# Modulation rows in a pool of their own, their sums queued behind evictions, and weights traced ahead of the forms

## The chip, the cores and the metric

The kernel runs on one core of a Trainium2 chip. The metric is the device time of one execution in microseconds (us). A core has five engines that run side by side, each working through its own instruction list in order: TensorE (PE, matrix products; PEld is its loading of stationary weights), VectorE (DVE, elementwise work), ScalarE (ACT, functions and copies), GpSimd (POOL) and SyncE (SP, which here issues nearly all DMA transfers). Products are accumulated in PSUM and brought back to SBUF by DVE or ACT; that step is called an eviction.

## The reference

A trunk of two layers works on one sequence of 512 tokens with 1024 channels. Layer 0 mixes tokens with a grouped complex state-space model (S5), layer 1 with forgetting attention (FoX, 16 heads of 64). Each is followed by a gated ConvFFN with 2816 hidden channels. So there are four sub-layers, numbered 0 to 3 in the kernel (S5, FFN0, FoX, FFN1), and each has this frame:

```python
shift, scale, gate = split(silu(c) @ ada_w + ada_b, 3)   # 3072 numbers from the 1024 of c
hn = rmsnorm(h, g) * (1 + scale) + shift
h = h + gate * sublayer(hn)
```

The attention adds to each logit the cumulated `log_sigmoid` of a forget logit. The FFN is `(silu(causal_conv3(a)) * b) @ w_down` with `a, b = split(hn @ w_up)`. All data are float32.

## The kernel before

**Products.** Activations lie with channels on the 128 partitions and tokens along the free dimension. Each float32 operand is split into a rounded part (`hi`, fp32r, made by ACT in line 286) and a remainder (`lo`, made by DVE in line 287; this is `put_parts`), and a product is three matmuls: hi·hi, hi·lo, lo·hi (`mms`, line 303). So each weight tile of 128x1024 costs one ACT copy (`w_hi`) and one DVE subtraction (`w_lo`) before TensorE can finish with it. Five buffers of each hold weights ahead of use (`WB`), three hold the raw loads.

**The FFN.** Its 22 hidden tiles f are handled in four groups of 6, 5, 6 and 5 (`GROUPS`); the down-projection of one group runs beside the up-projection of the next. A hidden tile is either *whole* (two up-products in halves, 96 matmuls with 256 columns) or *quartered* (`quarters`, line 523 on): seven products of a Winograd form, 84 such matmuls (line 558), for which DVE forms sums of weight quarters (line 529). The quartered tiles also need four sums of activations, the *forms* (`forms_x`: line 492 for the plain activations, line 498 for the differences), traced step by step beside the first whole tiles. `WHOLE_TILES` names the whole tiles of FFN0 and FFN1.

**The modulation sums.** For S5's shift and scale, and for FFN0's, TensorE multiplies `ada_w` by c (`ada_pe`). The other 64 rows of 128 values are made by DVE: `ada_units` loads a 128x1024 tile of transposed `ada_w` (`ada_raw`, 512 KB, by SP in line 254) and reduces its product with the row of c (`ada_c`) in line 255. Such a sum is called a sum or a row here. Generators with these sums stand in `self.bg`, and `tick(n)` traces n of them. `ada_pool` (line 242) opens room for the row of c and for 4 (S5), 2 (FFN0) or 3 (FoX) loads in the pool of the stage, and loads the row of c there, three times in all.

**Where the sums are traced.** S5's gate: three behind each of the last three GLU products (`ticks=3`). FFN0's gate, FoX's shift, scale and gate: in FFN0, by `SUMS`, 1 for each of tiles 0 to 3 and then 2. FFN1's shift, scale and gate: four behind each of two FoX value blocks (`self.tick(4)` in `fox_values`) and one behind each of the 16 q and k products.

**The order of work.** The start of S5 is ordered by hand. All else is ordered by a planner at compile time: it takes the program's order as priority, runs it against its own costs, and puts on each engine's list the first instruction that it expects to be ready. An instruction may so be listed far from its place in the program. A `behind(...)` block adds that an instruction must follow a named one on its engine's list.

**The forget logits.** `fox_values` computes the value tiles and, beside the first, the 16 forget logits `ft`. `log_forget` then runs a chain of about 40 small DVE instructions on them (lines 706 to 732, last result `lf_out`); `cumsum` transposes it on TensorE (line 1302), scans it on DVE (line 1306) and sends it through DRAM to the heads. On TensorE's list the transposes stand behind the value products, and the q and k products (line 303 again) behind the transposes.

Of the kernel before, what the change touches and what calls it, by code (L numbers as in the profile page):

```python
# [45 lines left out]
ROWS_FROM = 0  # L46
GROUPS = (6, 5, 6, 5)
TAIL = 4
WHOLE_TILES = (0, 1, 2, 3, 6, 8, 10, 12, 14, 16, 18), (0, 1, 2, 3)
SUMS = (1, 1, 1, 1, 2, 2) + (2,) * 12  # L50
FIRST = (("c", (KT,)), ("s5_prm", (3, G // 2)), ("s5_eye", (64,)))
REST = (
    ("ident", (P,)), ("ada_b", (4, 24)), ("norm_g", (4, KT)), ("final_g", (KT,)), ("cmask", (P,)), ("fox_bf", (NH,)), ("s5_causal", (L,)),
# [10 lines left out]
class Trunk:  # L64
# [6 lines left out]
    def __init__(self, tc, io, ctx):  # L71
        self.tc, self.nc, self.io, self.ctx = tc, tc.nc, io, ctx
        nc = self.nc
        pool = lambda name, bufs, **k: ctx.enter_context(tc.tile_pool(name=name, bufs=bufs, **k))
        self.const = pool("const", 1)
        self.act = pool("act", 1)
        self.wpool = pool("wpool", 3)
        self.tmp = pool("tmp", 2)
        self.small = pool("small", 2)
        self.dram = pool("dram", 1, space=DRAM)  # L80
        self.mm = pool("mm", 4, space=PSUM)
        self.aux = pool("aux", 4, space=PSUM)
        self.bg = []
        self.acc = None
        self.pending = None
        self.rests, self.odd = 0, False

        self.ones = self.const.tile([P, P], F32, name="ones")
        nc.vector.memset(self.ones, 1.0)
        self.sc = self.const.tile([P, KT], F32, name="sc")  # L90
        self.sc32 = self.const.tile([P, KT, 32], F32, name="sc32")

        self.sel = self.const.tile([P, 6], F32, name="sel")
        nc.gpsimd.memset(self.sel, 0.0)
# [144 lines left out]
        nc.scalar.activation(rows, ps, AF.Copy)  # L239
        nc.sync.dma_start(self.cd, rows)  # L240

    def ada_pool(self, pool, bufs):

        self.bgpool, self.ada_bufs = pool, bufs
        self.crow = pool.tile([P, D], F32, name="ada_c")
        self.nc.sync.dma_start(self.crow, self.cd.rearrange("k p -> (k p)")[None].to_broadcast([P, D]))

    def ada_units(self, i, thirds):

        nc = self.nc  # L250
        for t in thirds:
            for m in range(8 * t, 8 * t + 8):
                w = self.bgpool.tile([P, D], F32, name="ada_raw", bufs=self.ada_bufs)
                nc.sync.dma_start(w, self.io["ada_rows"][i - ROWS_FROM, m])
                nc.vector.tensor_tensor_reduce(  # L255
                    w, w, self.crow, 1.0, self.ada_b[:, i, m:m + 1], ALU.mult, ALU.add, self.par[i][:, m:m + 1]
                )
# [26 lines left out]
    def put_parts(self, hi, lo, src):  # L284
        nc = self.nc
        nc.scalar.activation(hi, src, AF.Copy)  # L286
        nc.vector.tensor_tensor(lo, src, hi.bitcast(F32), ALU.subtract)  # L287

    def weights(self, w, nk, *pool):

# [13 lines left out]
                o, wt, xt[:, cols], start=(k == 0 and n == 0), stop=(k == nk - 1 and n == 2),  # L304
            )

    def product(self, w, ms, nk, x, evac, head=0, tail=0, after=None, ticks=0, halves=HALVES, tail_pool=(), first=None, step=None, apart=False, ready=()):


        ms = list(ms)  # L310
        full = slice(0, S)
        if head:
            wk = first or {m: self.weights(w[m], nk) for m in ms[:head]}
            ps = {m: self.mm.tile([P, S], F32, name="mmp") for m in ms[:head]}
            for c in halves:
                for k in range(nk):
                    for m in ms[:head]:
                        self.mms(ps[m][:, c], wk[m], x, k, nk, c)
                    self.finish_norm((k + 1) * head)
                    if step:  # L320
                        step(3)
            for m in ms[:head]:
                evac(m, ps[m], full)
                self.tick(ticks)
        for m in ms[head:len(ms) - tail]:
            wk = ready[m] if m in ready else self.weights(w[m], nk)
            ps = self.aux.tile([P, S], F32, name="aux") if m in ready else self.mm.tile([P, S], F32, name="mmp")
# [39 lines left out]

    def add_residual(self, i, last=True):
        def evac(m, ps, cols):
            self.nc.vector.scalar_tensor_tensor(  # L370
                self.h[:, m, cols], ps, self.par[i][:, 16 + m:17 + m], self.h[:, m, cols],
                op0=ALU.mult, op1=ALU.add,
            )
            if last:
                self.square(m, cols)
# [213 lines left out]
    def ffn(self, i, l, x, nxt, whole, sums=()):  # L589

        nc, tc = self.nc, self.tc
        with tc.tile_pool(name=f"ffn{l}", bufs=1, reuse_waits="tile") as pool:
            if sums:
                self.ada_pool(pool, 2)
            first = [sum(GROUPS[:q]) for q in range(len(GROUPS) + 1)]
            keep, g = {}, {}

# [45 lines left out]
            todo = []  # L643
            for q, n in enumerate(GROUPS):
                for j, f in enumerate(range(first[q], first[q + 1])):
                    if f == 0:
# [1 line left out]
                        todo.append(self.forms_x(pool, x, b))  # L648
                    elif f in whole:
                        if f > 1:  # L650
                            up([f])
                        for _ in range(4):
                            if todo and next(todo[0], True):
                                todo.pop()
                    else:
# [131 lines left out]
class S5(Trunk):  # L787
# [291 lines left out]
    def s5(self, i, nxt):  # L1079
# [5 lines left out]
        with ExitStack() as stack:  # L1085
# [123 lines left out]
            for m in range(KT):  # L1209
# [24 lines left out]
                if m >= KT - 2:  # L1234
                    parts(m - 2)
            outputs(KT - 1)
            for k in range(KT - 1):
                if k == KT - 2:
                    parts(k)
                glu_head(k, 0)  # L1240
            for k in range(KT - 1):
                glu_head(k, 1)
            parts(KT - 1)
            for p in range(2):
                glu_head(KT - 1, p)
# [2 lines left out]
        with tc.tile_pool(name="s5b", bufs=1, reuse_waits="tile") as pool:  # L1248
# [5 lines left out]
            def glu(m, ps, cols):  # L1254
# [4 lines left out]

            self.product(  # L1260
                self.io["s5_w_glu"], range(HEAD, HEAD + 1), KT, (yhi, ylo), lambda m, ps, cols: gps.update({m: ps}),
                ready=ready,
            )
            for m in range(HEAD + 1):
                glu(m, gps[m], slice(0, S))
            self.ada_pool(pool, 4)
            self.bg = [self.ada_units(i, [2])]
            self.product(self.io["s5_w_glu"], range(HEAD + 1, KT), KT, (yhi, ylo), glu, ticks=3)
            self.load_x(resid)
            self.done()  # L1270
            after, y = nxt
            self.product(self.io["s5_w_out"], range(KT), KT, (zhi, zlo), self.add_residual(i), tail=2, after=after)
        return y


class Kernel(S5):
# [32 lines left out]
    def fox_values(self, pool, x):  # L1309
# [44 lines left out]
        values((0, 1), (0, 1), w)  # L1354
        values((0, 1), (2, 3), w, ((0, 2), (0, 3)))
        lf = self.log_forget(ft, pool)
        self.ada_pool(pool, 3)
        for q in range(2, NV):
            values((q,), range(NB), {q: load(q)})
            self.tick(4)  # L1360
        return lf

    def fox(self, i, x, nxt):
# [11 lines left out]
    def fox_heads(self, pool, x):  # L1375
# [14 lines left out]
        def project(m, ps, cols):  # L1390
            hi, lo = (pool.tile([P, S], F32R, name=n, tag="qk", bufs=QK) for n in ("hi", "lo"))
            if m % 2 == 0:
                sc = HD ** -0.5
                nc.scalar.activation(hi, ps, AF.Copy, scale=sc)
                nc.vector.scalar_tensor_tensor(lo, ps, sc, hi.bitcast(F32), op0=ALU.mult, op1=ALU.subtract)
                qp[m // 2] = hi, lo
            else:
                self.put_parts(hi, lo, ps)
# [103 lines left out]
def build(tc, io, out, stop=None):  # L1502
    with ExitStack() as ctx:
# [97 lines left out]
```

## Time and profile before

| | |
|---|---|
| median of 3 runs | 1236.39 us (1236.01 to 1238.03) |
| the profiled execution, its own time | 1235.54 us |
| its span, first to last instruction | 1233.8 us |
| TensorE busy | 1193.6 us (97%) |
| VectorE busy | 987.3 us (80%) |
| ScalarE busy | 597.2 us (48%) |
| modulation sums on VectorE | 64, 81.7 us |
| mean granted TensorE clock | 0.987 |

The profile times each instruction on its engine. A row of a timeline has the start, the duration, the engine, the line, what is written and read, and in brackets the idle time of the engine before it with what ended that. A row of the windows has a stretch of the span, its length, the busy time of PE, PEld, DVE, ACT and POOL with counts, the granted TensorE clock as a share of full speed, the busy share of the DMA engines and GB/s. A row of waits has the total idle time, the number of waits and the longest. In a row of the chain stand start, duration, what.

### The profile page before, as it was taken

How to read it: one execution, taken by the hardware profiler on the slowest of the kernel's cores; microseconds unless marked ns; L12 is line 12 of the kernel's file. 1: busy time of each engine (PE TensorE's matmuls, PEld its weight loads, DVE VectorE, ACT ScalarE, POOL GpSimd, SP SyncE). 2: the span in 40 equal slices, each digit the busy share in tenths (PEclk: the TensorE clock that was granted, in tenths of full speed). 3: DMA queues.
4: the chain of work that ended last, by engine and by line, in shares of the span. 5: the costliest groups of instructions: out<-in, count | busy, mean ns of one | idle time of the engine just before them, and what ended most of it. 6: DMA issues, size and time to landing. Idle time of an engine off the chain costs nothing.

```text
span 1233.8 us, 21319 instructions
## 1 busy us (share of the span) xinstructions
PE 1193.6 (97%) x8311; PEld 1042.2 (84%) x8311; DVE 987.3 (80%) x1824; ACT 597.2 (48%) x1102; POOL 57.0 (5%) x113
## 2 busy tenths in 40 slices
PE   7999998998999999999998899999989999999997
PEld 2566677898999999999898688888989999999987
DVE  7898977669998986667789777765899888888865
ACT  3544444435543444435443356654456555555543
POOL 0000000000000000000000234331000000000000
PEclk9999999999999999999999899999999999999999
DMA  9677559432566743323538734331313333333331
GB/s 360 225 238 226 140 177 331 158 124 84 184 221 221 241 133 108 107 77 103 181 120 312 244 109 133 128 104 39 101 56 108 117 108 92 116 103 108 103 86 69
DMA packets 73524, 184.92 MB, mean 150 GB/s; under 512 B 23135, under 2 KB 25535, under 8 KB 72399
## 3 DMA queue, kind: packets, MB, share of 16 engines
q1 hardware_dynamic: 73135, 183.04, 45.3%
q8 instruction: 65, 1.06, 0.4%
q10 hardware_dynamic: 288, 0.52, 0.1%
q14 instruction: 36, 0.29, 0.1%
HBM read 176.62 MB, written 6.92 MB: 149 GB/s over the span
## 4 chain that ended last, share of the span: by engine, by line
PE 87%; DVE 7%; DMA 3%; ACT 1%; issue 1%; SPq 0%; POOL 0%; DVEq 0%; ACTq 0%; POOLq 0%
PE mmp L303 44%; PE mmp L558 16%; PE aux L558 6%; PE mmp L1171 4%; PE mmp L1342 2%; PE aux L975 2%; PE aux L1488 2%; PE aux L1471 1%; DVE w_lo L287 1%; PE aux L1064 1%; PE aux L1056 1%; PE mmp L219 1%; DMA ada_raw<-in_ada_rows 1%; PE aux L1441 1%; DVE ada_raw L255 1%
## 5 line engine op out<-in xcount | busy, mean ns | idle before, releaser
L286 ACT ACTIVATE w_hi<-raw 128x1024 fp32r<-128x1024 f32 (+4 forms) x197 | 176.1, 902 | 170.3 <-PE mmp L303 87.6
L287 DVE TENSOR_TENSOR w_lo<-raw,w_hi 128x1024 fp32r<-128x1024 f32 (+4 forms) x197 | 203.5, 1037 | 31.5 <-ACT w_hi L286 30.8
L303 PE MATMUL mmp<-a_hi,w_lo 128*128 128x256 f32 (+1 forms) x632 | 195.2, 310 | 11.5 <-DVE w_lo L287 11.4
L303 PE MATMUL mmp<-a_hi,w_hi 128*128 128x256 f32 (+1 forms) x632 | 197.9, 315 | 0.5 <-DVE conv L614 0.5
L303 PE MATMUL mmp<-a_lo,w_hi 128*128 128x256 f32 (+1 forms) x632 | 194.5, 308 | 0.0
L303 PE MATMUL mmp<-ghi,w_hi 128*128 128x512 f32 (+1 forms) x392 | 143.9, 367 | 0.0
L303 PE MATMUL mmp<-glo,w_hi 128*128 128x512 f32 (+1 forms) x392 | 143.9, 367 | 0.0
L303 PE MATMUL mmp<-ghi,w_lo 128*128 128x512 f32 (+1 forms) x392 | 143.6, 366 | 0.0
L303 PEld LDWEIGHTS mmp<-a_hi,w_lo 128*128 128x128 f32 x632 | 121.1, 192 | 19.3 <-DVE w_lo L287 12.7
L303 PEld LDWEIGHTS mmp<-a_hi,w_hi 128*128 128x128 f32 x632 | 121.3, 192 | 8.6 <-issue 2.6
L303 PEld LDWEIGHTS mmp<-a_lo,w_hi 128*128 128x128 f32 x632 | 121.4, 192 | 5.1
L286 ACT ACTIVATE w_hi<-sums 128x1024 fp32r<-128x1024 f32 x66 | 69.6, 1059 | 57.2 <-DVE sums L529 27.8
L558 PE MATMUL mmp<-w_hi 128*128 128x256 f32 x348 | 96.1, 276 | 0.0
L558 PE MATMUL mmp<-w_lo,w_hi 128*128 128x256 f32 x348 | 96.1, 276 | 0.0
L558 PE MATMUL mmp<-w_hi,w_lo 128*128 128x256 f32 x348 | 96.0, 276 | 0.0
L255 DVE CUSTOM_DVE_ANT_0 ada_raw<-ada_raw,ada_c,rest 128x1024 f32<-128x1024 f32 x64 | 81.7, 1283 | 12.6 <-DMA ada_raw<-in_ada_rows 12.4
L287 DVE TENSOR_TENSOR w_lo<-sums,w_hi 128x1024 fp32r<-128x1024 f32 x66 | 80.1, 1220 | 12.1 <-ACT w_hi L286 11.0
L370 DVE SCALAR_TENSOR_TENSOR h<-mmp,par,h 128x512 f32<-128x512 f32 (+1 forms) x92 | 62.1, 677 | 32.1 <-PE mmp L303 32.0
L303 PEld LDWEIGHTS mmp<-ghi,w_lo 128*128 128x128 f32 x392 | 73.6, 188 | 12.3
L303 PEld LDWEIGHTS mmp<-ghi,w_hi 128*128 128x128 f32 x392 | 73.6, 188 | 11.2
L303 PEld LDWEIGHTS mmp<-glo,w_hi 128*128 128x128 f32 x392 | 73.6, 188 | 11.1
L558 PEld LDWEIGHTS mmp<-w_lo,w_hi 128*128 128x128 f32 x348 | 65.3, 188 | 0.0
(312 smaller groups left out, 2829.7 us busy)
## 6 DMA issues: line engine op xcount, KB each, us to landing
raw<-in_w_up SPq DMA_DIRECT2D x88, 512.0 KB, 3.6
ada_raw<-in_ada_rows SPq DMA_DIRECT2D x64, 512.0 KB, 4.7
raw<-in_ada_w SPq DMA_DIRECT2D x32, 512.0 KB, 6.5
raw<-in_w_down SPq DMA_DIRECT2D x32, 384.0 KB, 3.3
raw<-in_w_down SPq DMA_DIRECT2D x32, 320.0 KB, 3.0
nf<-nfd SPq DMA_DIRECT2D x8, 1152.0 KB, 5.7
raw<-in_fox_qk SPq DMA_DIRECT2D x16, 512.0 KB, 4.2
h<-in_x SPq DMA_DIRECT2D x8, 512.0 KB, 5.5
```

The lines of the kernel that those rows point to most:

```text
L219: self.last_mm = nc.tensor.matmul(ps[32 * qq:32 * qq + 32, :], self.sc32[:, k, :], w[:, q * S:(q + 1) * S], start=(step is steps[0]), stop ...
L255: nc.vector.tensor_tensor_reduce(w, w, self.crow, 1.0, self.ada_b[:, i, m:m + 1], ALU.mult, ALU.add, self.par[i][:, m:m + 1])
L286: nc.scalar.activation(hi, src, AF.Copy)
L287: nc.vector.tensor_tensor(lo, src, hi.bitcast(F32), ALU.subtract)
L303: self.last_mm = self.nc.tensor.matmul(o, wt, xt[:, cols], start=(k == 0 and n == 0), stop=(k == nk - 1 and n == 2),)
L370: self.nc.vector.scalar_tensor_tensor(self.h[:, m, cols], ps, self.par[i][:, 16 + m:17 + m], self.h[:, m, cols], op0=ALU.mult, op1=ALU.add,)
L558: self.last_mm = nc.tensor.matmul(o, wt[:, k], xt[:, k], start=(first and k == 0 and n == 0), stop=(k == H - 1 and n == 2), skip_group_che ...
L975: nc.tensor.matmul(ps[g2][:, j, cols], x[rows, a + j, r].rearrange("p c j -> p (c j)"), self.rr[rows, planes, q, :], start=(j == 0 and r = ...
L1056: nc.tensor.matmul(yp[g2][:, k, :], t[:, g].rearrange("p c i -> p (c i)"), u[:, g, :], start=(k == 0), stop=False, skip_group_check=True,)
L1171: nc.tensor.matmul(ps, w[m][:, k, :], x[:, k], start=(k == 0), stop=(k == KT - 1))
L1342: self.last_mm = nc.tensor.matmul(ps[q, b][:, :n], xt[:, k, tb], wt, start=(k == 0 and i == 0), stop=(k == KT - 1 and i == 2),)
L1488: nc.tensor.matmul(pv[:, c * P:], self.v[:, hp, k, r].rearrange("p t d -> p (t d)"), pp[:, r, c + 3 * k:NB + 3 * k, :].rearrange("p b t -> ...
```

## The change

- One pool `ada` lives from the start to the end, with the row of c and two loads of `ada_raw`. The row of c is loaded once, after the S5 outputs (`load_c`); `ada_pool` is gone.
- S5's gate sums are traced earlier: three after the first part of the GLU head, two after its second part, held behind the last step of the S5 scan, and one behind each of the last three GLU products.
- FFN0's gate sums move from FFN0 to S5's output product, two behind each of its tiles (`ticks=2`).
- FFN0 has no sums in tiles 0 to 5 and two in each of tiles 6 to 21; FFN1's gate sums move there from FoX. `fox_values` has none. The q and k products keep one each.
- `self.late` keeps the DVE instruction of the latest eviction (or remainder), and each sum must follow it on DVE's list.
- In both FFNs the weights of the next whole tile are traced ahead of the forms' steps while forms are left, and these get three steps a tile instead of four.
- FFN0 has 10 whole tiles instead of 11, placed otherwise.

```diff
-WHOLE_TILES = (0, 1, 2, 3, 6, 8, 10, 12, 14, 16, 18), (0, 1, 2, 3)
-SUMS = (1, 1, 1, 1, 2, 2) + (2,) * 12
+WHOLE_TILES = (0, 1, 2, 3, 4, 8, 11, 14, 17, 20), (0, 1, 2, 3)
+SUMS = (0,) * 6 + (2,) * 16
...
-        self.bg = []
+        self.bg, self.late = [], ()
...
+        self.ada = pool("ada", 1)
+        self.crow = self.ada.tile([P, D], F32, name="ada_c")
...
-    def ada_pool(self, pool, bufs):
-
-        self.bgpool, self.ada_bufs = pool, bufs
-        self.crow = pool.tile([P, D], F32, name="ada_c")
+    def load_c(self):
+
         self.nc.sync.dma_start(self.crow, self.cd.rearrange("k p -> (k p)")[None].to_broadcast([P, D]))
...
-                w = self.bgpool.tile([P, D], F32, name="ada_raw", bufs=self.ada_bufs)
+                w = self.ada.tile([P, D], F32, name="ada_raw", bufs=2)
                 nc.sync.dma_start(w, self.io["ada_rows"][i - ROWS_FROM, m])
-                nc.vector.tensor_tensor_reduce(
-                    w, w, self.crow, 1.0, self.ada_b[:, i, m:m + 1], ALU.mult, ALU.add, self.par[i][:, m:m + 1]
-                )
+                with self.behind(*self.late):
+                    nc.vector.tensor_tensor_reduce(
+                        w, w, self.crow, 1.0, self.ada_b[:, i, m:m + 1], ALU.mult, ALU.add, self.par[i][:, m:m + 1]
+                    )
...
-        nc.vector.tensor_tensor(lo, src, hi.bitcast(F32), ALU.subtract)
+        self.late = (nc.vector.tensor_tensor(lo, src, hi.bitcast(F32), ALU.subtract).ins,)
...
                     elif f in whole:
                         if f > 1:
-                            up([f])
-                        for _ in range(4):
+                            up([f], ready=ready)
+                            ready = {}
+                        if todo and f + 1 in whole:
+                            self.odd = True
+                            ready = {m: self.weights(self.io["w_up"][l][m], KT) for m in (2 * f + 2, 2 * f + 3)}
+                            self.odd = False
+                        for _ in range(3):
                             if todo and next(todo[0], True):
                                 todo.pop()
...
             outputs(KT - 1)
+            self.load_c()
+            self.bg, self.late = [self.ada_units(i, [2])], (self.scanned,)
             for k in range(KT - 1):
                 if k == KT - 2:
                     parts(k)
                 glu_head(k, 0)
+            self.tick(3)
             for k in range(KT - 1):
                 glu_head(k, 1)
+            self.tick(2)
             parts(KT - 1)
...
-            self.ada_pool(pool, 4)
-            self.bg = [self.ada_units(i, [2])]
-            self.product(self.io["s5_w_glu"], range(HEAD + 1, KT), KT, (yhi, ylo), glu, ticks=3)
+            self.product(self.io["s5_w_glu"], range(HEAD + 1, KT), KT, (yhi, ylo), glu, ticks=1)
             self.load_x(resid)
             self.done()
+            self.bg = [self.ada_units(i + 1, [2])]
             after, y = nxt
-            self.product(self.io["s5_w_out"], range(KT), KT, (zhi, zlo), self.add_residual(i), tail=2, after=after)
+            self.product(self.io["s5_w_out"], range(KT), KT, (zhi, zlo), self.add_residual(i), tail=2, after=after, ticks=2)
...
-        self.ada_pool(pool, 3)
         for q in range(2, NV):
             values((q,), range(NB), {q: load(q)})
-            self.tick(4)
...
-        k.bg = [k.ada_units(1, [2]), k.ada_units(2, [0, 1]), k.ada_units(2, [2])]
+        k.bg = [k.ada_units(2, [0, 1]), k.ada_units(2, [2]), k.ada_units(3, [2])]
         x = k.ffn(1, 0, x, k.norm_mod(2), WHOLE_TILES[0], SUMS)
...
-        k.bg = [k.ada_units(3, [0, 1]), k.ada_units(3, [2])]
+        k.bg = [k.ada_units(3, [0, 1])]
```

The evictions in `add_residual` and of q in the attention's `project` set `self.late` in the same way.

More of the change, by code (lines that the diff above doesn't have):

```diff
@@ L305, in mms, with product @@
             )
-    def product(self, w, ms, nk, x, evac, head=0, tail=0, after=None, ticks=0, halves=HALVES, tail_pool=(), first=None, step=None, apart=False, ready=()):
+    def product(self, w, ms, nk, x, evac, head=0, tail=0, after=None, ticks=0, halves=HALVES, tail_pool=(), first=None, step=None, apart=False, ready=(), spare=False):
         ms = list(ms)
@@ L326, in product @@
             wk = ready[m] if m in ready else self.weights(w[m], nk)
-            ps = self.aux.tile([P, S], F32, name="aux") if m in ready else self.mm.tile([P, S], F32, name="mmp")
+            ps = self.aux.tile([P, S], F32, name="aux") if spare else self.mm.tile([P, S], F32, name="mmp")
             for c in HALVES if apart else (full,):
@@ L369, in evac @@
         def evac(m, ps, cols):
-            self.nc.vector.scalar_tensor_tensor(
-                self.h[:, m, cols], ps, self.par[i][:, 16 + m:17 + m], self.h[:, m, cols],
-                op0=ALU.mult, op1=ALU.add,
+            self.late = (
+                self.nc.vector.scalar_tensor_tensor(
+                    self.h[:, m, cols], ps, self.par[i][:, 16 + m:17 + m], self.h[:, m, cols],
+                    op0=ALU.mult, op1=ALU.add,
+                ).ins,
             )
@@ L592, in ffn @@
         with tc.tile_pool(name=f"ffn{l}", bufs=1, reuse_waits="tile") as pool:
-            if sums:
-                self.ada_pool(pool, 2)
             first = [sum(GROUPS[:q]) for q in range(len(GROUPS) + 1)]
@@ L642, in ffn @@
             )
-            todo = []
+            todo, ready = [], {}
             for q, n in enumerate(GROUPS):
@@ L1261, in s5 @@
                 self.io["s5_w_glu"], range(HEAD, HEAD + 1), KT, (yhi, ylo), lambda m, ps, cols: gps.update({m: ps}),
-                ready=ready,
+                ready=ready, spare=True,
             )
@@ L1394, in project @@
                 nc.scalar.activation(hi, ps, AF.Copy, scale=sc)
-                nc.vector.scalar_tensor_tensor(lo, ps, sc, hi.bitcast(F32), op0=ALU.mult, op1=ALU.subtract)
+                self.late = (
+                    nc.vector.scalar_tensor_tensor(lo, ps, sc, hi.bitcast(F32), op0=ALU.mult, op1=ALU.subtract).ins,
+                )
                 qp[m // 2] = hi, lo
```

## The prediction, made before the change was run

> **What bounds the kernel now.** First the page: its head, the chain that ended last by engine, the sums' group and their loads.
>
> ```profile
> span 1233.8 us, 21319 instructions
> PE 1193.6 (97%) x8311; PEld 1042.2 (84%) x8311; DVE 987.3 (80%) x1824; ACT 597.2 (48%) x1102; POOL 57.0 (5%) x113
> PE 87%; DVE 7%; DMA 3%; ACT 1%; issue 1%; SPq 0%; POOL 0%; DVEq 0%; ACTq 0%; POOLq 0%
> ...
> L255 DVE CUSTOM_DVE_ANT_0 ada_raw<-ada_raw,ada_c,rest 128x1024 f32<-128x1024 f32 x64 | 81.7, 1283 | 12.6 <-DMA ada_raw<-in_ada_rows 12.4
> ...
> ada_raw<-in_ada_rows SPq DMA_DIRECT2D x64, 512.0 KB, 4.7
> ```
>
> TensorE is the bound: 40 us of the span are left that it is not busy. DVE comes next on the chain, and a sum holds DVE for 1.28 us. So I read TensorE's own waits, then its timeline where each long one ends.
>
> ```profile
> PE mmp L303 <- DVE w_lo L287: 11.4, 3, 4.8
> PE mmp L1302 <- DVE lf_out L732: 8.4, 1, 8.4
> ```
>
> ```profile
> 215.27 0.79 PE L303 MATMUL mmp<-a_hi,w_lo 128*128 128x512 f32 x1 [3.48 <-DVE w_lo L287]
> 308.80 0.58 PE L303 MATMUL mmp<-a_hi,w_lo 128*128 128x256 f32 x1 [4.78 <-DVE w_lo L287]
> 681.40 1.01 PE L1302 MATMUL mmp<-rest,lf_out 128*16 128x128 f32 x4 [8.36 <-DVE lf_out L732]
> 917.89 0.41 PE L303 MATMUL mmp<-a_hi,w_lo 128*128 128x256 f32 x1 [3.13 <-DVE w_lo L287]
> ```
>
> Four waits, 19.75 us, all for DVE: A in the last GLU products, B at FFN0's tile 3, C at the forget logits, D at FFN1's tile 3. The windows around them show a second price.
>
> ```profile
> 215.00:222.00 7.00, 6.73 (x23) 5.47 (x24) 5.37 (x8) 1.58 (x2) 0.00 (x0) 0.76 0.50 164
> 222.00:257.00 35.00, 35.00 (x166) 29.39 (x166) 20.77 (x23) 14.95 (x18) 0.00 (x0) 1.00 0.43 148
> 309.00:340.00 31.00, 31.00 (x254) 31.00 (x255) 30.78 (x45) 15.62 (x24) 0.00 (x0) 0.92 0.59 187
> 340.00:600.00 260.00, 260.00 (x1862) 243.09 (x1861) 204.05 (x296) 114.58 (x168) 0.12 (x1) 1.00 0.47 152
> 682.00:700.00 18.00, 18.00 (x87) 14.45 (x86) 12.29 (x18) 4.37 (x5) 2.54 (x2) 0.89 0.86 300
> 700.00:820.00 120.00, 118.86 (x696) 98.62 (x697) 86.72 (x226) 78.62 (x196) 44.62 (x68) 1.00 0.37 124
> 918.00:926.00 8.00, 8.00 (x57) 8.00 (x58) 7.62 (x10) 2.64 (x4) 0.00 (x0) 0.79 0.57 172
> 926.00:960.00 34.00, 34.00 (x294) 33.68 (x293) 33.14 (x49) 22.00 (x36) 0.00 (x0) 1.00 0.32 104
> ```
>
> Behind each wait the granted clock is low. A stretch of busy TensorE at a mean clock c loses length x (1 - c): 7 x 0.24 = 1.7, 31 x 0.08 = 2.5, 18 x 0.11 = 2.0, 8 x 0.21 = 1.7. So A costs 3.5 + 1.7 = 5.2 us, B 4.8 + 2.5 = 7.3, C 8.4 + 2.0 = 10.4, D 3.1 + 1.7 = 4.8; together 27.7.
>
> What DVE did ahead of each release, from its timeline (A, B, D; last column releasers):
>
> ```profile
> 210.34 1.32 DVE L255 CUSTOM_DVE_ANT_0 ada_raw<-ada_raw,ada_c,rest 128x1024 f32<-128x1024 f32 x1
> ...
> 212.75 1.32 DVE L255 CUSTOM_DVE_ANT_0 ada_raw<-ada_raw,ada_c,rest 128x1024 f32<-128x1024 f32 x1
> ...
> 213.95 1.26 DVE L287 TENSOR_TENSOR w_lo<-raw,w_hi 128x1024 fp32r<-128x1024 f32 x1
> ...
> 306.39 1.21 DVE L498 TENSOR_TENSOR sums<-x,x 128x1024 f32<-128x1024 f32 x1
> 307.53 2.35 DVE L287 TENSOR_TENSOR w_lo<-raw,w_hi 128x1024 fp32r<-128x1024 f32 x2
> ...
> 914.88 1.22 DVE L498 TENSOR_TENSOR sums<-x,x 128x1024 f32<-128x1024 f32 x1
> 916.01 0.68 DVE L287 TENSOR_TENSOR glo<-conv,ghi 128x512 fp32r<-128x512 f32 x1
> 916.62 1.22 DVE L287 TENSOR_TENSOR w_lo<-raw,w_hi 128x1024 fp32r<-128x1024 f32 x1
> ```
>
> At A the late weight remainder stands behind sums, at B and D behind the forms. For C, DVE over the whole chain of the forget logits: all of it, then the sums (each counts twice, with its read-out), then remainders and evictions of line 287.
>
> ```profile
> 652.00:681.10 29.10, 27.77 (x75) 0.91 0.87 305
> ...
> 652.00:681.10 29.10, 14.11 (x22) 0.91 0.87 305
> ...
> 652.00:681.10 29.10, 10.57 (x15) 0.91 0.87 305
> ```
>
> Eleven sums took 14.1 of these 29.1 us; what else there is takes 13.7.
>
> **The change, part by part.** *Sums out of the value blocks (C).* Without them DVE's 13.7 us of other work end near 652 + 13.7 = 666. TensorE asked at 681.40 - 8.36 = 673.0, so 7 us of cover remain and the wait goes: -10.4. Late next would be the first scores, which need the scan and two transfers behind the transposes; that is a rival below.
>
> *Sums out of the GLU (A) and FFN0's start (B).* The windows of line 255 alone:
>
> ```profile
> 195.00:214.00 19.00, 7.86 (x12) 1.00 0.86 310
> ...
> 265.00:290.00 25.00, 3.84 (x6) 1.00 0.52 171
> ```
>
> At A the weights would have to be ready 3.5 us sooner. Six sums stood ahead of them; five of S5's eight move forward and at most one or two stay ahead, so at least four, 5.1 us, go: -5.2. At B three sums go, 3.8 us, two tiles' weights come ahead of the forms, and tile 4, now whole, asks DVE for two remainders instead of a quartered tile's sums; 4.8 us are needed: -7.3. Tiles 5, 6 and 7 are now quartered in a row. From 309 to 340 two such tiles in a row kept DVE full (30.78 of 31) and TensorE never idle; a third with sums I price at 0 to 2.6 (its two sums), and take 0.5.
>
> *Where these five go.* Behind the last scan step DVE makes the remainders of the GLU head.
>
> ```profile
> 177.85 4.62 DVE L1198 TENSOR_TENSOR w_lo<-raw,w_hi 128x1024 fp32r<-128x1024 f32 x4
> ```
>
> ```profile
> 185.32 6.51 PE L1201 MATMUL mmp<-a_hi,w_lo 128*128 128x512 f32 x28
> ```
>
> They are ready at 182.5 and read from 185.3 on: 2.9 us of cover. Two or three sums in front take 2.6 to 3.8, so 0 to 1.0 us appear, and more if SP stands before a row whose buffer isn't free with the reads of y queued behind it, at most one landing, 4.7. The room issues nothing itself, and two of three loads of the row of c fall away. I take 0.5, near the case without a blocked queue, since the first two rows find their buffers free.
>
> *FFN0's gate sums in the output product.* Eight, 10.2 us, beside 222 to 257, where DVE has 14.2 us idle and TensorE none: 0.
>
> *One whole tile fewer.* 96 - 84 = 12 matmuls, which this row of the chain has as
>
> ```profile
> 431.84 1.36 PE aux L558 x12
> ```
>
> so -1.4. *Sums in tiles 6 to 21*: 32 in place of 24, spread over the rest of FFN0; 340 to 600 has 56 us of idle DVE and TensorE never idle: 0.
>
> *Attention.* 16 sums behind the evictions of q and k; the trace had one of them after 700. They put DVE at 86.7 + 19.2 = 106 of 120 us. Bounds: -1.1 (the idle time there goes) to +19.2 (all on the path); I take +0.5, nearest to FFN0's row, as DVE keeps 14 us.
>
> *FFN1's start (D).* Weights come ahead of the forms, but DVE's work is the same, and it is full to 960. So the question is what is late next: the first quartered tile's sums.
>
> ```profile
> 924.29 1.23 DVE L287 TENSOR_TENSOR w_lo<-sums,w_hi 128x1024 fp32r<-128x1024 f32 x1
> ```
>
> ```profile
> 930.23 2.49 PE mmp L558 x22
> ```
>
> Ready at 925.5, read by that tile's second product at 930.2 + 1.4 = 931.6: 6.1 us of cover. TensorE would come 4.8 earlier, which leaves 1.3; but tile 3's evictions, four steps of about 0.7 (as the 0.68 at 916.01), also come earlier and stand in front, 2.8. So 0 to 1.5 us come back, or all 4.8 if order wasn't it. I take 1.3: -3.5.
>
> Sum: -5.2 - 7.3 - 10.4 - 3.5 - 1.4 + 0.5 + 0.5 + 0.5 = -26.3. The profiled execution took 1235.5 by its own time and the median is 1236.4; so 1209.2 against the first, 1210 against the second.
>
> [...]
>
> **The rivals.** *FFN1's wait only moves* (for: DVE at 33.14 of 34 behind it; against: 6.1 us of cover): -26.3 + 3.5, 1214.
>
> *The first scores wait.* TensorE's first scores, and what DVE did with them:
>
> ```profile
> 697.69 0.38 PE L1441 MATMUL aux<-hi 64*128 64x256 f32 x2
> ```
>
> ```profile
> 699.96 1.28 DVE L255 CUSTOM_DVE_ANT_0 ada_raw<-ada_raw,ada_c,rest 128x1024 f32<-128x1024 f32 x1 [2.18 <-DMA ada_raw<-in_ada_rows]
> ...
> 701.17 0.28 DVE L1453 CUSTOM_DVE_ANT_0 s<-aux,nf 128x128 f32<-128x128 f32 x1
> ```
>
> For: from the transposes at 681.4 DVE's first score took 19.8 us; transposes at 673 give 693, while TensorE, without the 2.0 of half clock, offers scores 14.3 us behind them, at 687. Against: a sum that waited 2.2 us for its row stood before that score. Price up to 6 us: 1216.
>
> *It doesn't do what it says*: the planner still lists weights late, since a sum is tied to one instruction only. Then the tile alone remains: 1235.
>
> *Rows late at the head of DVE's list* (slower). Eleven of 64 sums waited for their load, 12.4 us, 1.1 each, at up to four buffers; now there are two everywhere, and remainders and evictions queue behind a waiting sum. If all 32 pairs wait 1.1 us and TensorE feels it, +35.2: 1236.4 - 26.3 + 35.2 = 1245. It decides above 26.3 / 32 = 0.8 us a pair. Against: with two buffers FFN0 ran 24 sums, and TensorE had no idle time from 340 to 600.
>
> **How the numbers follow.** Forecast 0.55; FFN1 moves 0.17; first scores 0.13; nothing 0.07; slower 0.08. The likeliest is 1210. Low: all gains without costs, -29.1, give 1207, and 3 us beneath for other short waits: 1204. High: both middle rivals together and the 3 us that a late y or a third sum may add: 1222. Outside lie about 0.17: nothing, slower, and a little of the rest. A measurement of this kernel can tell 0.2%, 2.5 us: faster 0.85 (the first three), same 0.07 (1235 is 1.4 from the median), slower 0.08.
>
> **What would show it.** Right: no wait of TensorE on w_lo or lf_out over 1 us, granted clock 1.00 in the stretches above, value blocks without line 255, 84 x 12 = 1008 quarter matmuls in FFN0, and line 255 spread to FFN0's end. Wrong: waits of line 1201 on w_lo, of line 1441 or 1471 on DVE or POOL, DVE idle for ada_raw well over 12.4 us, or a wait at FFN1's first quartered tile.

## The result, and the profile after

The changed kernel takes 1207.41 us (1205.89 to 1209.27, 4 runs) where the kernel before takes 1236.89 (1236.01 to 1238.03, 4 runs): a ratio of 0.9762, with a 95% interval of 0.9744 to 0.978. The forecast was 1210, in a range of 1204 to 1222. The profiled execution took 1206.57 us by its own time, 29.0 less than the one before.

The page of the changed kernel: its head, the chain that ended last by engine, and the group of the sums, which are now on line 256 (lines of the prediction have moved by one to ten).

```profile
span 1204.6 us, 21290 instructions
...
PE 1184.1 (98%) x8299; PEld 1034.5 (86%) x8299; DVE 994.2 (83%) x1834; ACT 600.7 (50%) x1108; POOL 60.7 (5%) x113
...
PE 83%; DVE 8%; DMA 4%; ACT 2%; issue 2%; POOL 0%; SPq 0%; DVEq 0%; ACTq 0%; POOLq 0%
...
L256 DVE CUSTOM_DVE_ANT_0 ada_raw<-ada_raw,ada_c,rest 128x1024 f32<-128x1024 f32 x64 | 83.6, 1326 | 2.5 <-DMA ada_raw<-in_ada_rows 2.4
```

TensorE is idle for 20.5 us where it was 40.2, has 12 matmuls fewer, and DVE stands idle for rows 2.4 us in place of 12.4. What TensorE still waits for, longest first:

```profile
PE mmp L1116 <- ACT nm_t L1115: 5.8, 1, 5.8
PE mmp L1146 <- DVE a_x L1132: 1.7, 1, 1.7
PE aux L390 <- DVE ssq L365: 1.1, 1, 1.1
```

The first two lie in the first 28 us, and the kernel before had both (6.3 and 1.1). The waits on w_lo and on lf_out, 19.75 us together, are gone. The stages in which A, B, C and D lay, by windows (columns: PE, PEld, DVE, ACT, POOL, then granted clock, DMA share, GB/s); the last but one is the attention, of which more below:

```profile
195.00:222.00 27.00, 27.00 (x121) 22.36 (x120) 25.27 (x29) 15.58 (x23) 0.00 (x0) 1.00 0.80 280
...
260.00:320.00 60.00, 60.00 (x527) 59.75 (x526) 57.07 (x95) 33.08 (x48) 0.00 (x0) 1.00 0.24 78
...
652.00:700.00 48.00, 47.44 (x280) 39.49 (x279) 30.76 (x73) 24.76 (x58) 15.75 (x19) 1.00 0.50 167
674.50:794.50 120.00, 119.44 (x702) 98.86 (x699) 100.34 (x250) 78.52 (x196) 47.85 (x69) 1.00 0.55 181
870.00:960.00 90.00, 89.56 (x732) 87.11 (x732) 87.50 (x120) 53.47 (x79) 0.00 (x0) 1.00 0.30 97
```

The clock is 1.00 in each. The span is 29.2 us shorter, and of that TensorE's idle time makes 19.7, as much as the four waits (19.75), and its busy time 9.5. Of the 9.5, 1.36 are the 12 matmuls of the whole tile, by the price of the prediction (no run took this part alone); 8.1 are left for the half clock behind the four waits, which the prediction had summed to 7.9.

### The profile page after: what moved, and what is told of

It is laid out like the page before. It is cut to its first block, busy times and chain, and to the rows that moved or that the text cites. A ratio compares the mean times of both kernels' runs of the same rounds, so it can differ in the third digit from the quotient of the medians.

```text
span 1204.6 us, 21290 instructions
## 1 busy us (share of the span) xinstructions
PE 1184.1 (98%) x8299; PEld 1034.5 (86%) x8299; DVE 994.2 (83%) x1834; ACT 600.7 (50%) x1108; POOL 60.7 (5%) x113
## 3 DMA queue, kind: packets, MB, share of 16 engines
q8 instruction: 65, 1.06, 0.4%
## 4 chain that ended last, share of the span: by engine, by line
PE 83%; DVE 8%; DMA 4%; ACT 2%; issue 2%; POOL 0%; SPq 0%; DVEq 0%; ACTq 0%; POOLq 0%
PE mmp L304 41%; PE mmp L561 14%; PE aux L561 5%; PE mmp L1351 3%; PE mmp L1177 3%; DVE w_lo L288 2%; PE mmp L1207 2%; PE aux L981 2%; PE aux L1497 2%; PE aux L1480 1%; PE aux L1062 1%; PE aux L1070 1%; DMA raw<-in_w_up 1%; PE mmp L221 1%; DVE sums L532 1%
## 5 line engine op out<-in xcount | busy, mean ns | idle before, releaser
L304 PE MATMUL mmp<-a_hi,w_hi 128*128 128x256 f32 (+1 forms) x600 | 185.9, 311 | 0.0
L304 PE MATMUL mmp<-a_hi,w_lo 128*128 128x256 f32 (+1 forms) x600 | 182.8, 306 | 0.0
L304 PE MATMUL mmp<-a_lo,w_hi 128*128 128x256 f32 (+1 forms) x600 | 182.6, 305 | 0.0
L304 PEld LDWEIGHTS mmp<-a_hi,w_hi 128*128 128x128 f32 x600 | 112.4, 188 | 7.6 <-issue 2.5
L304 PEld LDWEIGHTS mmp<-a_hi,w_lo 128*128 128x128 f32 x600 | 112.5, 188 | 6.4
L304 PEld LDWEIGHTS mmp<-a_lo,w_hi 128*128 128x128 f32 x600 | 112.6, 188 | 4.8
L561 PE MATMUL mmp<-w_hi 128*128 128x256 f32 x360 | 99.6, 277 | 0.2 <-ACT nm_h L568 0.2
L561 PE MATMUL mmp<-w_hi,w_lo 128*128 128x256 f32 x360 | 99.5, 276 | 0.0
L561 PE MATMUL mmp<-w_lo,w_hi 128*128 128x256 f32 x360 | 99.4, 276 | 0.0
L561 PEld LDWEIGHTS mmp<-w_hi 128*128 128x128 f32 x360 | 67.6, 188 | 0.5 <-ACT nm_h L568 0.4
```

Of the source, the lines that this page charges most:

```text
L304: self.last_mm = self.nc.tensor.matmul(o, wt, xt[:, cols], start=(k == 0 and n == 0), stop=(k == nk - 1 and n == 2),)
L561: self.last_mm = nc.tensor.matmul(o, wt[:, k], xt[:, k], start=(first and k == 0 and n == 0), stop=(k == H - 1 and n == 2), skip_group_che ...
```

## The experiments

Twelve kernels were run, each against the kernel before on the same chip. Beside these kernels the median of the kernel before lies at 1234.7 to 1236.9, so they are compared by their ratios: a difference of 0.001 is 1.24 us, and the difference of two ratios is uncertain by about 0.002 to 0.003.

| kernel | what differs | median us | ratio | 95% interval |
|---|---|---|---|---|
| changed kernel | all of the change | 1207.41 | 0.9762 | 0.9744 to 0.978 |
| e1_values | FFN1's gate sums written in the value blocks, not held | 1206.32 | 0.9758 | 0.9743 to 0.9772 |
| e2_nohold | no sum held | 1227.32 | 0.993 | 0.9906 to 0.9954 |
| e3_notahead | no weights ahead of the forms | 1209.62 | 0.9784 | 0.9769 to 0.9799 |
| e4_glu | S5's gate sums back in the last GLU products | 1213.00 | 0.9812 | 0.979 to 0.9835 |
| e1c_forget | 16 sums ahead of the forget logits' chain | 1222.03 | 0.989 | 0.9874 to 0.9906 |
| e6_first | sums back in FFN0's first tiles | 1211.07 | 0.9811 | 0.9793 to 0.9829 |
| e9_four | no weights ahead, four steps of the forms | 1217.26 | 0.9855 | 0.984 to 0.987 |
| e10_holdonly | the kernel before, with the hold alone | 1227.81 | 0.9941 | 0.9926 to 0.9956 |
| e11_fourahead | weights ahead, four steps | 1207.82 | 0.9779 | 0.9766 to 0.9793 |
| i1_seven | seven whole tiles in FFN0 | 1205.55 | 0.9759 | 0.974 to 0.9777 |
| e7_nosums | no sums at all | 1204.41 | 0.976 | 0.9737 to 0.9783 |
| i3_five | five whole tiles in FFN0 | 1217.35 | 0.9852 | 0.9836 to 0.9868 |

**Places without the hold, and the hold without the places.** The first kernel is the changed one with

```
-                with self.behind(*self.late):
+                with self.behind():
```

> The changed kernel with all its places for the sums, but no sum is held behind an eviction or the scan. Theory, the places did it: the planner takes a few sums earlier, no long wait of TensorE comes back, 1207 to 1210. Rival, the hold did it: sums slip in front of the weights wherever a row has landed, in FFN0's first tiles above all, and one or two of the waits of 5 to 10 us come back, 1212 to 1222.

It took 1227.32 (its profiled execution 1230.90): without the hold, 0.017 or some 21 us of the gain are lost. The group of the sums (duration in ns, then first and last start) tells why; first of this kernel, then of the kernel before, then of the changed one.

```profile
L256 DVE CUSTOM_DVE_ANT_0 ada_raw<-ada_raw,ada_c,rest x64: 1271/1281/1337, 141.8 to 497.1; 128x1024 f32<-128x1024 f32 x64
```

```profile
L255 DVE CUSTOM_DVE_ANT_0 ada_raw<-ada_raw,ada_c,rest x64: 1248/1278/1349, 195.6 to 700.0; 128x1024 f32<-128x1024 f32 x64
```

```profile
L256 DVE CUSTOM_DVE_ANT_0 ada_raw<-ada_raw,ada_c,rest x64: 1267/1279/1711, 176.5 to 799.3; 128x1024 f32<-128x1024 f32 x64
```

With a room that is open throughout and no hold, all 64 sums are done by 498 us, those written into the attention too: the planner lists them as early as it can. Eight of them now stand between 254 and 279 us, in the normalization ahead of FFN0, in front of the sum of squares and of the root that TensorE waits for. The longest waits behind the start (first fence) and the two stretches of lowest clock (second, columns as above):

```profile
PE mmp L561 <- ACT nm_h L568: 4.4, 5, 3.0
PE aux L420 <- DVE rs_y L411: 3.9, 2, 3.7
PE aux L390 <- DVE ssq L365: 3.6, 1, 3.6
```

```profile
167.00:179.00 12.00, 11.70 (x61) 10.18 (x62) 12.00 (x20) 4.91 (x10) 0.33 (x4) 0.57 0.31 88
262.00:285.00 23.00, 16.02 (x90) 15.59 (x91) 17.02 (x52) 6.48 (x12) 0.00 (x0) 0.70 0.59 198
```

In the first stretch, the last scan steps of S5, two sums run, at 174.0 and 176.5, and the wait is 1.7 us for ACT and ends at 167.3, so they are not its cause; what is, isn't shown. The 3.0 us on nm_h end at 465.1 in FFN0, 10 us behind a sum that itself stood 2.8 us for its row at the head of DVE's list; over the 64 sums such waits are 13.2 us here and 2.4 in the changed kernel, both with two loads.

The other kernel is the one before, with its places, rooms, tiles and forms, and only the hold added:

```
-                nc.vector.tensor_tensor_reduce(...)
+                with self.behind(*self.late):
+                    nc.vector.tensor_tensor_reduce(...)
...
-        nc.vector.tensor_tensor(lo, src, hi.bitcast(F32), ALU.subtract)
+        self.late = (nc.vector.tensor_tensor(lo, src, hi.bitcast(F32), ALU.subtract).ins,)
```

(and the same in the evictions of the residual and of q).

> The kernel before, with one thing of the change alone: each sum held behind the eviction that was traced last. Its places, its rooms, its tiles and its forms stay. Theory (the hold is most of the change, since unheld sums run as early as their room is open, wherever they are written): A and C shrink or go, D (4.8 us) stays and B in part, two sums still stand ahead of the forms: 1217 to 1224. Rival (places are most of it): lf_out and w_lo are waited for as before, 1230 to 1236.

It took 1227.81, 7.3 us less than before by its ratio and a little above the range expected. Its long waits:

```profile
224.69 0.49 PE L304 MATMUL mmp<-zhi,w_hi 128*128 128x512 f32 x1 [1.99 <-ACT zhi L287]
...
309.11 0.58 PE L304 MATMUL mmp<-a_hi,w_lo 128*128 128x256 f32 x1 [5.50 <-DVE w_lo L288]
...
696.88 1.49 PE L1472 MATMUL aux<-rest,s 128*128 128x128 f32 x4 [3.31 <-POOL s L1463]
...
911.56 0.39 PE L304 MATMUL mmp<-a_hi,w_lo 128*128 128x256 f32 x1 [3.09 <-DVE w_lo L288]
```

C is gone by the hold alone: no wait on lf_out is left. Three sums stand right in front of lf_out, where eleven stood in the 29 us of its chain before, and it is ready at 667.4, 6.1 us ahead of the transposes. But three more stand in front of the scan behind them (674.5 to 678.1), and 3.3 us come back at the first scores, 23 us behind the transposes (673.6), as the second rival of the prediction had it. A has moved to the output product's first operand (zhi), D is as long as it was, and B rather longer. So the hold alone is worth 0.6%, the rest of the change without the hold 0.7%, and both together 2.4%: each needs the other.

**C, the forget logits.** A first attempt put the eight sums back into the value blocks, not held there, and took them out of FFN0 (the edit in part):

```
...
         for q in range(2, NV):
             values((q,), range(NB), {q: load(q)})
+            self.hold = False
+            self.tick(4)
+            self.hold = True
...
```

> The changed kernel, but FFN1's gate sums stand again in the two value blocks of the attention, four behind each and not held, and FFN0 has them no longer. Theory: the sums stand between the steps of the forget logits on VectorE's list, so TensorE's wait at the transposes comes back with its half clock: a wait of 7 to 9 us there and 1207 + 10.4 = 1217 to 1219. Rival, the wait came from other things that changed too (the loads, the order of the weights): under 1 us of wait and 1207 to 1209.

It took 1206.32, against the theory. The windows of line 256 in it say why it is no test of C:

```profile
500.00:560.00 60.00, 15.22 (x24) 1.00 0.60 203
560.00:600.00 40.00, 0.00 (x0) 1.00 0.50 151
600.00:652.00 52.00, 0.00 (x0) 1.00 0.21 72
652.00:681.00 29.00, 3.01 (x4) 1.00 0.49 164
```

(Each sum counts twice, with its read-out.) From 560 on only 16 sums are left, as many as the q and k products have; so the eight written into the value blocks ran before 560, beside FFN0, for the same reason as all sums of the run without the hold. A second attempt holds 16 sums at the logits, and lists them ahead of their chain:

```
+                    self.late = (nc.vector.tensor_tensor(ft[:, b, :], ps[q, b][:, W:W + NH], bf, ALU.add).ins,)
+                    self.asked = self.late
...
+        self.late = self.asked
+        self.tick(16)
         lf = self.log_forget(ft, pool)
```

> The last layer's 16 shift and scale sums move from the attention to the forget logits: held behind the addition that makes the logits, and listed ahead of their chain, so that 11 of them stand in DVE's list between that addition and lf_out (none do in the changed kernel). Theory (C was the sums' place: lf_out was ready 8.4 us before TensorE asked, and 11 sums of 1.25 us take 13.8): TensorE waits about 5 us on lf_out and then has a halved clock for one or two stretches, 2 to 3 us more: 1213 to 1216. Rival (DVE has room there, and TensorE does not feel it once sums are held): no wait, 1206 to 1209.

It took 1222.03, 15.8 us over the changed kernel by ratio: the theory's side, and about twice its size.

```profile
640.00:673.00 33.00, 13.99 (x22) 0.92 0.76 268
...
667.60:678.00 10.40, 4.74 (x14) 0.51 0.67 236
...
673.26 1.01 PE L1311 MATMUL mmp<-rest,lf_out 128*16 128x128 f32 x4 [10.80 <-DVE lf_out L738]
```

The eleven sums take 14.0 us, near the 13.8 expected, but lf_out ends at 673.1, 22.7 us later than in the changed kernel: two sums also waited for their rows (0.69 and 1.78 us), and remainders of weights and of v that stood behind the chain got ahead of it. After the wait of 10.8 the clock stays at half for another 4.5 us, which loses 2.2; a wait of 2.02 us on ssq at 604 (1.05 in the changed kernel) and a stretch of half clock behind it (0.54 from 605.9 to 609.6) lose 2.7 more. Together that is 15.7.

**A, the gate sums of S5.** All eight go back into the last GLU products, held (lines between left out):

```
-            self.bg, self.late = [self.ada_units(i, [2])], (self.scanned,)
...
-            self.tick(3)
...
-            self.tick(2)
...
-            self.product(self.io["s5_w_glu"], range(HEAD + 1, KT), KT, (yhi, ylo), glu, ticks=1)
+            self.bg = [self.ada_units(i, [2])]
+            self.product(self.io["s5_w_glu"], range(HEAD + 1, KT), KT, (yhi, ylo), glu, ticks=3)
```

> The changed kernel, but S5's eight gate sums stand in the last three GLU products again, three behind each, held behind evictions as in the changed kernel. Theory: VectorE makes the weights' remainders there too late again, a wait of 3 to 4 us with half a window of half clock, +5.2: 1212. Rival, being held behind evictions is enough for the remainders to pass: 1207 to 1208.

It took 1213.00, 6.2 us over by ratio, near the theory's price. But the wait is another one:

```profile
223.17 0.50 PE L304 MATMUL mmp<-zhi,w_hi 128*128 128x512 f32 x1 [2.20 <-ACT zhi L287]
224.30 0.50 PE L304 MATMUL mmp<-zlo,w_hi 128*128 128x512 f32 x1 [0.63 <-DVE zlo L288]
...
224.70:228.30 3.60, 3.60 (x11) 0.53 0.87 291
```

Held sums stand behind the remainder that TensorE needs in the GLU, and in front of the elementwise steps that make zhi and zlo, which the output product needs; one of them stood 1.4 us for its row, at 217.1. That is 2.8 us and 1.7 of clock, 4.5 in all.

**B and D, the first tiles of the FFNs.** The change has three parts here: no sums, weights ahead of the forms, and three steps of the forms behind a whole tile in place of four. The prediction read over the third. One kernel leaves out the weights ahead (`if False:` in place of `if todo and f + 1 in whole:`), one takes four steps (`range(4)`), one does both, and one puts the sums back (`SUMS = (1, 1, 1, 1, 2, 2) + (2,) * 12`).

> The changed kernel, but the next whole tile's weights are not traced ahead of the forms; the forms keep three steps a tile. Theory: FFN1's wait at tile 3 comes back in full, 4.8 us, and a part of FFN0's, where no sums stand any more, 0 to 3: 1212 to 1215. Rival, the three steps do it alone: 1206 to 1209 and no wait over 1 us at either place.

It took 1209.62: 2.7 us over the changed kernel by ratio, about what two such ratios can tell apart, and there is no wait on w_lo at any tile 3.

> Four steps of the forms behind each whole tile as before the change, and no weights ahead of them; sums as in the changed kernel. Theory (D was the forms standing ahead of the late weight remainder, and B half so): TensorE waits about 3 us on w_lo at FFN1's tile 3, with 1.7 us of clock behind it, and 1 us or less at FFN0's: 1212 to 1215. Rival (the order of the forms is worth no more than the 2.2 us that the weights alone were): 1208 to 1211.

It took 1217.26, 11.5 us over by ratio, and here both waits are back (timeline, then windows of TensorE alone):

```profile
301.08 0.39 PE L304 MATMUL mmp<-a_hi,w_lo 128*128 128x256 f32 x1 [3.30 <-DVE w_lo L288]
...
607.87 0.61 PE L390 MATMUL aux<-ones,ssq 128*128 128x1 f32 x4 [1.39 <-DVE ssq L365]
...
899.91 0.58 PE L304 MATMUL mmp<-a_hi,w_lo 128*128 128x256 f32 x1 [3.13 <-DVE w_lo L288]
```

```profile
302.50:306.00 3.50, 3.50 (x19) 0.51 0.75 274
609.50:613.50 4.00, 4.00 (x24) 0.57 0.00 2
900.00:903.50 3.50, 3.50 (x17) 0.53 0.53 167
```

D is back to the hundredth (3.13 before, 3.13 here). B is back at 3.30 of its 4.78, though no sum stands there: the theory had given it 1 us or less, and the time lies above its range.

> Four steps of the forms behind each whole tile as before the change, with the weights ahead of them as in the changed kernel: the other half of the run without either, which took 1217.3 with two waits on w_lo of 3.3 and 3.1 us. Theory (three steps in place of four carry B and D, the weights ahead hardly anything): TensorE waits 2 to 3 us on w_lo at tile 3 of each FFN, with a stretch of half clock behind each: 1213 to 1217. Rival (either of the two is enough, each puts tile 3's late remainder ahead of the last forms): no such wait, 1206 to 1210.

The rival is right: 1207.82, 0.0017 over the changed kernel and not told apart from it, with no wait on w_lo. So either of the two is enough, weights ahead or one step less, and the change has both.

> FFN0's sums are spread as before the change (one beside each of tiles 0 to 3, two from tile 4 on), each still held behind an eviction; weights ahead of the forms and the three steps stay. Theory (B was the three sums ahead of the forms): four sums, 5 us, are back ahead of the first quartered tile, TensorE waits 2 to 5 us there or at tiles 3 and 4 and loses 2 to 3 us of clock: 1212 to 1215. Rival (the weights ahead of the forms cover it): 1206 to 1209.

It took 1211.07, 6 us over by ratio with ±3, between the two. Tile 3 runs without a wait; the sums cost at the first quartered tile, some 45 us later:

```profile
348.02 0.39 PE L561 MATMUL mmp<-w_hi,w_lo 128*128 128x256 f32 x1 [1.98 <-DVE w_lo L288]
...
349.00:353.00 4.00, 4.00 (x23) 0.57 0.83 286
```

With a wait of 0.94 us on w_hi at 343.7 that is 2.9 and 1.7.

**What the sums still cost.** This kernel has none, and leaves out what its expectation says:

> Without the 64 sums and the loads of their rows: these modulation rows are only their bias, the part made from c is left out. It shows what the sums still cost. Theory (all are hidden now, as the windows with TensorE never idle say): 1204 to 1208. Rival (their share of DVE, 84 us, and of the transfers, 32 MB, still holds TensorE up in short waits or by contention): 1196 to 1203.

By ratio, 0.976 against 0.9762, the sums and their loads cost nothing that can be measured, to within 0.003 or some 4 us. Beyond that nothing is to be had from moving them.

**A version that might be faster still.** Where TensorE is never idle, fewer whole tiles save matmuls. First `(0, 1, 2, 3, 4, 9, 15)`, then `(0, 1, 2, 3, 4)` in place of FFN0's ten whole tiles:

> Seven whole tiles in FFN0 in place of ten (0 to 4, 9 and 15), three more quartered; nothing else. The term of the whole tile (12 matmuls of 0.113 us each) gives 3 x 1.36 = 4.1 us, if DVE keeps up: it was busy 254.9 of 300 us from 300 to 600. Theory: no new wait of TensorE, 1203 to 1204.5. Rival (a quartered tile with its two sums asks more of DVE than TensorE's time for it, so four or five in a row run out of the lead): waits of TensorE on line 561, 1206 to 1212.

> Only tiles 0 to 4 of FFN0 whole: two quartered tiles more than in the run with seven, which took 1205.55 with DVE at 270.4 and TensorE at 298.2 of the 300 us from 300 to 600. 5 x 1.36 = 6.8 us of matmuls fewer than in the changed kernel. Theory (DVE, some 5 us more per quartered tile, reaches 280 of 300 and TensorE waits in short pieces on its sums and conversions): 2 to 5 us of waits on line 561, so 1202 to 1206, no clear gain over seven. Rival (DVE still has room): 1200 to 1202. Second rival (a wait that halves the clock): over 1207.

Seven took 1205.55 (ratio 0.9759): 1.9 us less in the medians, and by ratio the same as the changed kernel, where 4.1 were to be had. Five took 1217.35, 11 us worse (its profiled execution took 1222.85). FFN0 from 300 to 600, first with seven, then with five and its worst part, in windows:

```profile
sum 300.00, PE 298.17 PEld 279.10 DVE 270.42 ACT 148.98 POOL 0.52; mean PE 49.69 PEld 46.52 DVE 45.07 ACT 24.83 POOL 0.09
```

```profile
460.00:520.00 60.00, 52.74 (x372) 48.61 (x372) 51.89 (x80) 27.50 (x44) 0.00 (x0) 1.00 0.42 142
...
sum 300.00, PE 290.22 PEld 270.65 DVE 272.52 ACT 148.41 POOL 0.52; mean PE 48.37 PEld 45.11 DVE 45.42 ACT 24.73 POOL 0.09
```

With seven, TensorE has begun to wait, 1.8 of 300 us. With five it loses 9.8, but DVE is not full either, 272.5 and not the 280 that the theory had: from 460 to 520 both stand still for some 8 us. What holds both there was not settled; in that window DVE waits 4.2 us for rows of w_up, ACT 5.6, and ACT another 7.0 for DVE's sums of weight quarters. SP, which issues the loads, stands 22.0 of these 60 us in front of loads of ada_raw, whose two buffers are still held by sums that have not run, with the loads of w_up and w_down behind them. That fits late weights (over the 300 us such waits of SP are 84.1, and 65.0 in the changed kernel), but no run took it away. Of the two numbers tried, seven is where this ends.

## Why the prediction was right, step by step

*The four waits.* All of A, B, C and D went, with their half clocks: 27.7 was predicted, 27.9 came (19.75 of waits and 8.1). The reading that each of the four costs its length and a stretch of half clock behind it carries more than a quarter of the gain (8.1 of 29.2 us).

*C's cover.* The prediction had lf_out ready at 666 and asked for at 673, 7 us of cover. In the changed kernel:

```profile
650.12 0.23 DVE L738 SCALAR_TENSOR_TENSOR lf_out<-lf_ring 128x64 f32<-128x64 f32 x1
...
658.70 0.60 PE L1311 MATMUL mmp<-rest,lf_out 128*16 128x128 f32 x4
...
675.79 0.29 DVE L1462 CUSTOM_DVE_ANT_0 s<-aux,nf 128x128 f32<-128x128 f32 x1 [1.17 <-POOL nf L1428]
```

It is 8.3 us, and eleven sums in front overrun it, as the run with held sums at the logits shows. But the reason given, "Sums out of the value blocks", is only half of it. What counts is how many sums stand ahead of lf_out on DVE's list, and their place in the program does not decide that alone: the run with the hold alone lost this wait with the sums still written there, and the run without the hold had no place that meant anything.

*B.* The step "three sums go, 3.8 us, two tiles' weights come ahead of the forms" named the right end by the wrong weights. With the sums gone and the forms as before, 3.30 of 4.78 us stay: the sums, together with the hold and the whole tile 4, were worth 1.5 at tile 3, and the order of forms and weights the rest.

*D.* The step that failed is "I take 1.3: -3.5". Nothing came back at the first quartered tile: TensorE is busy 89.56 of 90 us from 870 to 960. The order of the forms was the whole of D, as four steps without weights ahead bring it back at 3.13. The prediction credited the weights ahead and read over the step from four to three, which alone does the same.

*A.* Gone as predicted. Its price when the sums go back, 4.5 us by the trace, is near the 5.2 taken, though at another wait.

*The costs.* 0.5 each was taken for the S5 join, the quartered tiles in a row and the attention; all three are nothing. At the join three sums do stand in front, as counted, and the last remainder ends at 185.9, 1.6 us after TensorE has begun the products that read them; it comes to that one late enough not to wait:

```profile
183.49 2.38 DVE L1204 TENSOR_TENSOR w_lo<-raw,w_hi 128x1024 fp32r<-128x1024 f32 x2
...
184.22 6.59 PE L1207 MATMUL mmp<-a_hi,w_lo 128*128 128x512 f32 x28
```

In the attention DVE rose from 86.7 to 100.3 us of 120 (106 was expected), in windows that start as far ahead of DVE's first score (700.0 to 820.0 before, 674.5 to 794.5 after), and TensorE's busy time from 118.86 to 119.44. These 1.5 and D's 1.3 are why 1210 lies 2.6 us over the result; "all gains without costs", 1207, was the truth.

*The rivals.* FFN1's wait did not move. The first scores did not wait: DVE's first score came 17.1 us behind the transposes, not 19.8, and TensorE lost 0.6 us there. That rival is real all the same, since the hold alone meets it with 3.3 us. "The planner still lists weights late" was met by the hold: tied to one instruction, the sums did stand where they were put. The slower rival needed rows late at the head of DVE's list; they were late by 2.4 us over all 64 sums, in place of 12.4, with fewer buffers. It did show where sums ran at other places: 13.2 us in the run without the hold.

## What to carry to other kernels

Work that a planner lists goes as early as its buffers allow, wherever it is written: to move it, tie it to an instruction, and look in the trace for the first and last start of its group before believing a place. A tied piece stands in front of something too, so ask which eviction or remainder is now behind it (here zhi, and the first scores). And put each part of a change back alone and together with its neighbour, since two parts that each suffice, or each fail alone, look the same in one run.

## What the runs showed of the hardware

A wait far shorter than the stretch of half clock behind it halved TensorE's clock in one run, and a longer one in another run did not. In the run with four steps, with TensorE busy throughout, three stretches of half clock lost 1.7 us each: 3.5 x 0.49, 4.0 x 0.43 and 3.5 x 0.47 in its windows, so they lasted 3.4. One of them came behind a wait of 1.39 us (607.87 in that run). In other runs such a stretch came behind 1.98, with one of 0.94 four us earlier (sums back in FFN0's first tiles), and behind 2.20 and 0.63 together (S5's sums back in the GLU). It did not come behind a wait of 1.76 in the kernel without weights ahead:

```profile
603.73 0.60 PE L390 MATMUL aux<-ones,ssq 128*128 128x1 f32 x4 [1.76 <-DVE ssq L365]
...
602.00:612.00 10.00, 8.18 (x69) 1.00 0.04 16
```

nor behind 1.05 in the changed kernel. In the wait of 10.8 us the clock halved while TensorE still stood, and only what was left when it started again cost time: 10.4 us at 0.51 from 667.6 on, of which TensorE was busy for 4.7.

Most of this goes with where the wait falls. The traces record the granted clock with the times of its changes, and within each trace all changes lie a whole number of 3.41 us apart; the pieces of 3.41 us on that grid are called windows here. In the kernel before, the stretches of half clock at the four waits run from 214.96, 307.12, 675.76 and 918.11 and last 3.41, 6.83, 10.24 and 3.41 us: one, two, three and one such windows. The wait of 1.39 lies within one window, and the next ran at half clock; the longer one of 1.76 is shared by two windows, with 1.06 us idle in one and 0.71 in the other, and the clock stayed full (rows of the run with four steps, then of the one without weights ahead):

```profile
606.36:609.78 3.42, 2.03 (x19) 1.92 (x17) 1.31 (x4) 0.83 (x2) 0.00 (x0) 1.00 0.05 20
609.78:613.19 3.41, 3.41 (x17) 3.41 (x17) 2.29 (x13) 0.42 (x1) 0.00 (x0) 0.50 0.01 2
...
599.61:603.02 3.41, 2.35 (x21) 2.16 (x20) 2.00 (x5) 1.06 (x3) 0.00 (x0) 1.00 0.53 183
603.02:606.44 3.42, 2.71 (x23) 2.71 (x24) 1.31 (x6) 0.61 (x2) 0.00 (x0) 1.00 0.02 8
```

Over all 14 traces, from 200 us to 12 us before the end, each of the 19 full-clock windows in which TensorE stood for 1.92 us or more was followed by half clock, and none in which it stood for 1.22 or less. Between lie six: 1.30, 1.39 and 1.63 halved the clock, 1.38, 1.64 and 1.77 did not. The three that did are all waits on ssq, between matmuls of 128x1; whether so small ones count for less was not tried.
